# Twelve lower parts of the weights made by accumulating transfers instead of VectorE

## The chip, the cores and the metric

The kernel runs on one core of one Trainium2 chip. The metric is the device time of one launch in microseconds (us). A profile is one execution seen by the hardware profiler; its span runs from the core's first instruction to its last.

## The reference

Two layers, each on 256 tokens of width 1024. A layer normalizes its input, multiplies it by one wide input projection, feeds the columns of that product to three token mixers, projects each mixer's output to the model width, merges the three by gates and adds the result to its input:

```
h = rms_norm(x, norm_g)
proj = jnp.einsum('btd,de->bte', h, w_in)
(qa, ka, va, za, ba, aa, ub, zb, qc, kc, vc, zc, iq, ik, iw, gates) = split_columns(proj)
ya = deltanet_branch(qa, ka, va, za, ...)      # gated delta rule, short convolution on q, k, v
yb = pooling_branch(ub, zb, pool_w, pool_scale)
yc = sparse_attention_branch(qc, kc, vc, zc, iq, ik, iw, ...)
projected = jnp.einsum('btnc,ncd->btnd', branches, w_branch)
merged = jnp.sum(gate * projected, axis=2)
return x + jnp.einsum('btd,de->bte', merged, w_out)
```

All of it is float32.

## The kernel before

Large products are done in a reduced float format (`F32R`) in three products instead of one: a weight w is split into an upper part `wh` (w rounded to the reduced format) and a lower part `wl` = w - wh, the activations likewise into `hh` and `hl`, and TensorE adds up wh·hh, wh·hl and wl·hh. So each block of weights of 128x1024 float32 numbers (512 KB) passes four stations, written in `wslot`: a transfer that SyncE issues fills a buffer of `raw`; ScalarE (or VectorE) casts it into a buffer of `wh`; VectorE subtracts `wh` from `raw` into a buffer of `wl`; TensorE multiplies. There are 5 buffers of `raw`, 6 of `wh` and 5 of `wl`.

```
plan.add("ACT", "copy", (h[:, :n], raw[:, :n]), {}, ("DVE", "tensor_copy"))
V.tensor_tensor(lo[:, :n], raw[:, :n], h[:, :n].bitcast(F32), op=ALU.subtract)
```

The columns that a mixer wants with channels on the partitions go through `proj_cm`: ZC (the sparse attention's gate), KA, QA and VA (the delta rule's k, q and v), UB and ZB (the pooling mixer). Each of the six is four blocks of 128 columns; a call of `proj_cm` makes two of them in one PSUM bank of the kind `pj`. A block is 24 matmuls of 256 columns: 8 with hh,wh, 8 with hl,wh and, last, 8 with hh,wl. The calls stand in the order ZC, ZC, KA, QA, KA, QA, VA, VA, UB, UB, ZB, ZB. This part of a layer is called the channel stretch below: about 52 to 136 us in the first layer and about 320 to 411 us in the second. The other large products (`proj_tm`, `by_token`, `outp`) have 512 columns.

Nothing is issued where it is written. `Plan.add` records each operation, and `Plan.lay_out` replays all of them with a table of costs, engine by engine, and so fixes the order of each engine's queue and the buffer of each tile; it may also move a copy from ScalarE to VectorE (the last argument of `plan.add` above). A change of one operation's engine or cost therefore moves many others. On the chip each engine works its queue in that order and waits where an input is not there.

GpSimd (POOL) has little to do: some memsets, small powers (`rsqrt`, the tiles r4k, r4q, rk, so, rs) and two transfers of constants near the start. A transfer issued from it is listed under the queue POOLq.

Of the kernel before, what the change touches and what calls it, by code (L numbers as in the profile page):

```python
# [9 lines left out]
F32 = mybir.dt.float32  # L10
F32R = mybir.dt.float32r
AF = mybir.ActivationFunctionType
ALU = mybir.AluOpType
# [77 lines left out]


_slots()


def lay_w_in(w):
# [172 lines left out]
class Plan:  # L269
# [35 lines left out]
    def cost(self, eng, call, args, kw):  # L305


        out = args[0]
        n = int(np.prod(out.shape[1:])) if len(out.shape) > 1 else 1
        if call == "dma_start":  # L310
            run = int(args[1].shape[-1]) * 4
            rate = 120.0 if run < 512 else 262.0 if run < 1024 else 318.0 if run < 4096 else 338.0
            return 550.0 if eng == "POOL" else 475.0, n * out.shape[0] * 4 / rate, False
        if eng == "PE":
            if call == "transpose":
                return 109.0, 170.0, False
            if args[1].ap.dtype == F32R:
                return (n / 2.4 + 13.3 if n > 100 else 60.0), 175.0, False
            m, k = args[1].shape[-1], args[1].shape[0]
            if k <= 32:  # L320
                return 16.0, 170.0, False
            if k <= 64:
                return 58.0 * max(n / 64.0, 1.0), 170.0, False
            return 2 * (max(n, m) / 1.2 + 3), 170.0, False
        srcs = [a for a in args[1:] if isinstance(a, Ref)]
        space = [r.tile.tag.psum for r in srcs]
        ps = any(space)
        w = max([int(np.prod(r.shape[1:])) for r in srcs] + [n])
        acc = kw.get("accum_out") is not None
        if eng == "ACT":  # L330
            hold = (18 if ps else 78) + 0.875 * w
            if isinstance(kw.get("bias"), Ref) or isinstance(kw.get("scale"), Ref):
                hold += 100
            return hold + (120 if acc else 0), (95 if ps else 22) + (90 if acc else 0), False
        if eng == "POOL":
            if kw.get("op") == ALU.pow:
                return 405.0 + 151 * n, 10.0, False
            if call == "memset":
                return 50 + 0.8 * n, 50.0, False
            return 90 + 2.2 * w, 60.0, True  # L340
        if call == "reciprocal":
            return 70 + 6.0 * w, 80.0, False
        fast = call in ("tensor_copy", "tensor_scalar") and not ps and not out.tile.tag.psum
        hold = 66 + (0.52 if fast or call == "memset" else 1.045) * w
        if call in ("scalar_tensor_tensor", "tensor_scalar") and any(isinstance(a, Ref) for a in args[2:3]):
            hold += 58
        if call == "stream_shuffle":
            hold += 40
        if call == "transpose":
            hold = 464.0  # L350
        two = [r for r in ([args[1], args[2]] if call == "tensor_tensor" else
                           [args[1], args[3]] if call == "scalar_tensor_tensor" else [])]
        port = fast or (bool(two) and not any(isinstance(r, Ref) and r.tile.tag.psum for r in two))
        return hold + (65 if acc else 0), 80.0 + (30 if acc else 0), port
# [83 lines left out]
    def lay_out(self):  # L438
# [112 lines left out]
        while len(order) < len(self.ops):  # L551
            best = None
            for e in engines:
                c = pick(e)
                if c and (best is None or c[:2] < best[:2]):
                    best = c
            if best is None:
                left = [o for o in self.ops if o.start is None]
                raise RuntimeError(f"the plan is stuck with {len(left)} operations left, the first: "
                                   f"{left[0].eng} {left[0].call} {left[0].n}")  # L560
            at, e, q = best
            o = self.ops[q[1]]
            if e == "POOL" and o.other and free["DVE"] < at + PATIENCE:
                now[e] = [p for p in now[e] if p != q]
                heapq.heapify(now[e])
                soon[e] = [p for p in soon[e] if p[1:] != q]
                heapq.heapify(soon[e])
                continue
            got = slots(o)
            if got is None:  # L570
                continue
            if max(got, o.est) > at + 1e-6:
                now[e] = [p for p in now[e] if p != q]
                heapq.heapify(now[e])
                soon[e] = [p for p in soon[e] if p[1:] != q]
                heapq.heapify(soon[e])
                heapq.heappush(soon[e], (max(got, o.est), rank(o, e), o.n, o.turn))
                continue
            if o.other and e == o.other[0]:
                o.eng, o.call, o.cost, o.tail, o.port = o.other  # L580
            for t in o.tiles:
                if t.slot is None:
                    g = t.tag
                    f = min(g.free)
                    g.free.remove(f)
                    t.slot = f[1]
                    if t.slot in g.held:
                        g.held[t.slot].then = t
                    g.held[t.slot] = t
                    while g.next < len(g.order) and g.order[g.next].slot is not None:  # L590
                        g.next += 1
                    if g.free:
                        again, g.parked = g.parked, []
                        for p in again:
                            ready(p)
            if e in ("DVE", "ACT"):
                for z in o.tiles:
                    if z.tag.psum:
                        z.reader, z.until = e, at + o.cost + o.tail + 36.0
            o.start = at  # L600
            if e == "PE":
                part = fill(o) < 0.6
                free[e] = clock.run(at, o.cost + (SWITCH if part != small else 0.0), fill(o))
                if small and not part:
                    whole = at
                small = part
            else:
                free[e] = at + o.cost
            if e in shared and o.port:
                shared[e] = free[e] + (15 if e == "DVE" else 60)  # L610
            o.end = free[e] + o.tail
            if o.call == "dma_start":
                dma_free = max(dma_free, at + (2500.0 if e == "POOL" else 1360.0)) + o.tail
                o.end = dma_free + 600.0 + (DELAY if at > CALM else EARLY)
            order.append(o)
            for d in o.outs:
                d.wait -= 1
                if e == "PE" and d.eng == "PE":
                    d.est = max(d.est, at)
                else:  # L620
                    d.est = max(d.est, o.end + (35.0 if e == d.eng else self.LAG[d.eng] + (MARGIN if d.eng == "PE" else 0)))
                if not d.wait:
                    ready(d)
            for t in o.tiles:
                t.left -= 1
                t.end = max(t.end, o.end + 60)
                if not t.left:
                    g = t.tag
                    g.free.append((t.end, t.slot))
                    again, g.parked = g.parked, []  # L630
                    for p in again:
                        ready(p)
# [15 lines left out]
def trunk(ctx: ExitStack, tc: tile.TileContext, x, xt, gain, w_in, gate_b, pool_w, w_branch, w_out, cst0, cst1, cst2, cst3,  # L648
# [122 lines left out]
        G.tensor_tensor(dst, src, mhalf[:, :src.shape[-1]], op=ALU.pow)  # L771


    def wslot(src, shape, raw=None):
        n = shape[0] * shape[1]
        if raw is None:
            raw = make("raw", [128, 1024], F32)
# [1 line left out]
        h = make("wh", [128, 1024], F32R)  # L779
        lo = make("wl", [128, 1024], F32R)  # L780
        plan.add("ACT", "copy", (h[:, :n], raw[:, :n]), {}, ("DVE", "tensor_copy"))
        V.tensor_tensor(lo[:, :n], raw[:, :n], h[:, :n].bitcast(F32), op=ALU.subtract)
        return (h[:, :n].rearrange("p (k c) -> p k c", k=shape[0]),
                lo[:, :n].rearrange("p (k c) -> p k c", k=shape[0]))

# [14 lines left out]
            tabs[l, name] = c_t, s_t  # L800

    for l in range(DEPTH):
        def w_slot(key, shape):
            n = shape[0] * shape[1]
            return wslot(bass.AP(tensor=w_in.tensor, offset=w_in.offset + l * WIN + SLOT[key], ap=[[n, 128], [1, n]]),
                         shape)


        grow = grows[l]
# [71 lines left out]
        def proj_cm(c0):  # L881
            ps = bank("pj")
            o = v2(ps)
            for b in range(2):
                wh, wl = w_slot(("cm", c0 + b * 128), (8, 128))
                seq = [(w, hx, k) for w, hx in ((wh, hh), (wh, hl), (wl, hh)) for k in range(KB)]
                for n, (w, hx, k) in enumerate(seq):
                    mm(o[:, b, :], w[:, k, :], hx[:, k, :], n == 0, n == len(seq) - 1)
# [633 lines left out]
```

## Time and profile before

| | |
|---|---|
| time, median of 3 runs | 559.20 us (559.17 to 559.31) |
| time of the profiled execution | 559.21 us |
| its span | 557.4 us |
| TensorE (PE) busy | 552.3 us, 99% |
| VectorE (DVE) busy | 502.3 us, 90% |
| ScalarE (ACT) busy | 323.0 us, 58% |
| GpSimd (POOL) busy | 24.4 us, 4% |
| data moved | 99.79 MB, 179 GB/s |

The profiled execution took 1.8 us more than its span, which lies ahead of and behind the instructions. Busy shares are means over the whole span. PEld is TensorE's loading of weights into its array, which overlaps its matmuls. Idle time in a row is put down to the instruction that ended it (the releaser).

### The profile page before, as it was taken

The page shows a single profiled execution, that of the slowest core. Times are in us where ns is not written, and L with a number is a line of the kernel's source. Part 1 is how long each engine was busy: PE and PEld are TensorE (multiplying, and loading weights), DVE is VectorE, ACT ScalarE, POOL GpSimd, SP SyncE. Part 2 cuts the span into 40 slices and gives each one's busy share as a digit, 9 for nine tenths or more (in the row PEclk, how much of TensorE's full clock was granted, in tenths as well). Part 3 has the DMA queues.
Part 4 walks back from the last instruction along what each step waited for, and adds up shares of the span by engine and source line. Part 5 has one row for each costly group of instructions (what it writes and reads, how often), then busy time and mean ns, then how long its engine had stood idle before and what let it go on. Part 6 is the DMA issues. An engine that isn't in the chain of part 4 may idle for free.

```text
span 557.4 us, 9530 instructions
## 1 busy us (share of the span) xinstructions
PE 552.3 (99%) x3430; PEld 485.7 (87%) x3430; DVE 502.3 (90%) x1115; ACT 323.0 (58%) x654; POOL 24.4 (4%) x31
## 2 busy tenths in 40 slices
PE   9999999999999999999999999999999999999997
PEld 7978999999888887888879789999988888788886
DVE  6999999999999999687699999999999999967662
ACT  7795775867654526553476765765584444445530
POOL 0300000001000000000010020001000000000000
PEclk9999999999999999999999999999999999999999
DMA  8854565471866654534447446436456666346402
GB/s 327 312 194 152 186 205 183 126 268 49 308 210 194 230 181 161 199 132 152 149 142 231 138 144 202 141 127 225 133 183 215 202 207 213 119 149 208 156 33 76
DMA packets 29855, 99.79 MB, mean 179 GB/s; under 512 B 3312, under 2 KB 4080, under 8 KB 29808
## 3 DMA queue, kind: packets, MB, share of 16 engines
q1 hardware_dynamic: 29232, 98.22, 53.2%
q0 software_dynamic: 288, 0.64, 0.4%
q8 instruction: 27, 0.44, 0.3%
q10 hardware_dynamic: 288, 0.33, 0.2%
q14 instruction: 20, 0.16, 0.1%
HBM read 98.12 MB, written 1.05 MB: 178 GB/s over the span
## 4 chain that ended last, share of the span: by engine, by line
PE 89%; DVE 7%; issue 1%; ACT 1%; DMA 1%; POOL 0%; DVEq 0%; POOLq 0%
PE pj L643 72%; PE mx L643 17%; DVE u L643 2%; DVE wl L643 1%; DVE score L643 1%; DVE big L643 1%; DVE top L643 1%; DMA x_sb<-in_xt_dram 1%; ACT big L643 1%; POOL rk L643 0%; ACT wh L643 0%; DVE hl L643 0%; DVE x_sb L643 0%; ACT u L643 0%; ACT hh L643 0%
## 5 line engine op out<-in xcount | busy, mean ns | idle before, releaser
L643 ACT CAST wh<-raw 128x1024 fp32r<-128x1024 f32 (+2 forms) x165 | 170.7, 1040 | 133.0 <-PE pj L643 104.7
L643 DVE TENSOR_TENSOR wl<-raw,wh 128x1024 fp32r<-128x1024 f32 (+2 forms) x176 | 209.1, 1198 | 9.9 <-PE pj L643 5.3
L643 PE MATMUL pj<-wh,hh 128*128 128x512 f32 (+1 forms) x352 | 103.2, 391 | 0.3 <-ACT wh L643 0.3
L643 PE MATMUL pj<-wh,hl 128*128 128x512 f32 (+1 forms) x352 | 101.6, 389 | 0.0
L643 PE MATMUL pj<-wl,hh 128*128 128x512 f32 (+1 forms) x352 | 100.8, 386 | 0.0
L643 PEld LDWEIGHTS pj<-wh,hh 128*128 128x128 f32 x352 | 64.6, 188 | 13.5 <-issue 0.7
L643 PEld LDWEIGHTS pj<-wl,hh 128*128 128x128 f32 x352 | 65.1, 188 | 12.9 <-DVE wl L643 0.6
L643 PEld LDWEIGHTS pj<-wh,hl 128*128 128x128 f32 x352 | 64.8, 188 | 12.2 <-DVE hl L643 0.4
L643 PE MATMUL pj<-hh,wl 128*128 128x256 f32 x384 | 56.3, 285 | 0.0
L643 PE MATMUL pj<-hh,wh 128*128 128x256 f32 x384 | 55.3, 285 | 0.0
L643 PE MATMUL pj<-hl,wh 128*128 128x256 f32 x384 | 55.3, 285 | 0.0
L643 PE MATMUL pj<-wh,y 128*128 128x512 f32 (+1 forms) x208 | 51.5, 383 | 0.0
L643 PEld LDWEIGHTS pj<-hh,wl 128*128 128x128 f32 x384 | 50.3, 192 | 0.0
L643 PEld LDWEIGHTS pj<-hh,wh 128*128 128x128 f32 x384 | 50.2, 192 | 0.2
L643 PEld LDWEIGHTS pj<-hl,wh 128*128 128x128 f32 x384 | 49.9, 192 | 0.0
L643 PEld LDWEIGHTS pj<-wh,y 128*128 128x128 f32 x208 | 38.5, 188 | 7.5
L643 PE MATMUL mx<-wh,y 128*128 128x512 f32 (+1 forms) x128 | 38.4, 380 | 0.0
L643 PEld LDWEIGHTS mx<-u,u 128*128 128x128 f32 (+2 forms) x336 | 29.1, 164 | 3.0 <-issue 1.1
L643 PE MATMUL mx<-u,u 128*128 128x128 f32 (+2 forms) x336 | 30.7, 250 | 0.0
L643 DVE SCALAR_TENSOR_TENSOR u<-pj,cs,u 128x255 f32<-128x255 f32 (+2 forms) x72 | 29.3, 470 | 0.4 <-ACT u L643 0.4
L643 PE MATMUL pj<-wl,y 128*128 128x512 f32 (+1 forms) x104 | 28.5, 382 | 0.0
L643 PEld LDWEIGHTS mx<-wh,y 128*128 128x128 f32 x128 | 23.3, 188 | 4.4 <-DVE y L643 0.2
(202 smaller groups left out, 682.3 us busy)
## 6 DMA issues: line engine op xcount, KB each, us to landing
raw<-in_w_in_dram SPq DMA_DIRECT2D x124, 512.0 KB, 4.2
raw<-in_w_branch_dram SPq DMA_DIRECT2D x24, 512.0 KB, 4.4
raw<-in_w_out_dram SPq DMA_DIRECT2D x16, 512.0 KB, 3.5
tg<-in_gate_b_dram SPq DMA_DIRECT2D x12, 256.0 KB, 4.8
raw<-in_w_in_dram SPq DMA_DIRECT2D x4, 498.0 KB, 6.1
raw<-in_xt_dram SPq DMA_DIRECT2D x4, 256.0 KB, 4.2
raw<-in_xt_dram SPq DMA_DIRECT2D x2, 512.0 KB, 5.8
x_sb<-in_x_dram SPq DMA_DIRECT2D x2, 512.0 KB, 5.0
```

Source lines behind the costliest of these rows:

```text
L643: getattr(self.real[o.eng], o.call)(*[put(a) for a in o.args], **{k: put(v) for k, v in o.kw.items()})
```

## The change

In each of the six channel projections the last block of four is prepared in another way, twelve blocks in all over the two layers. ScalarE writes the negated weights into the buffer of the lower part; since that buffer has the reduced format, what arrives is the negated upper part. Then POOL issues a transfer from `raw` into that buffer that adds to what stands there: -wh + w = wl. VectorE's subtraction is left out for these blocks. The cast into `wh` stays. The table of costs gets a rate and a delay for such a transfer.

```diff
+def adds(l, block):
+    return block % 4 == 3
...
-            rate = 120.0 if run < 512 else 262.0 if run < 1024 else 318.0 if run < 4096 else 338.0
+            rate = 180.0 if kw.get("accum_op") is not None else 120.0 if run < 512 else 262.0 if run < 1024 else 318.0 if run < 4096 else 338.0
...
-                o.end = dma_free + 600.0 + (DELAY if at > CALM else EARLY)
+                o.end = dma_free + 600.0 + (DELAY if at > CALM else EARLY) + (1500.0 if o.kw else 0.0)
...
-    def wslot(src, shape, raw=None):
+    def wslot(src, shape, raw=None, adding=False):
...
-        V.tensor_tensor(lo[:, :n], raw[:, :n], h[:, :n].bitcast(F32), op=ALU.subtract)
+        if adding:
+            S.activation(lo[:, :n], raw[:, :n], AF.Copy, scale=-1.0)
+            G.dma_start(lo[:, :n], raw[:, :n], accum_op=ALU.add)
+        else:
+            V.tensor_tensor(lo[:, :n], raw[:, :n], h[:, :n].bitcast(F32), op=ALU.subtract)
...
-                wh, wl = w_slot(("cm", c0 + b * 128), (8, 128))
+                wh, wl = w_slot(("cm", c0 + b * 128), (8, 128), adds(l, c0 // 128 + b))
```

Counted over the whole program, VectorE has 12 subtractions of 128x1024 fewer (166 to 154) and 5 casts `wh<-raw` of 128x1024 more (10 to 15), and a few smaller copies more; ScalarE has the 12 negations and 5 such casts fewer (156 to 151), and those smaller copies fewer; POOL has the 12 transfers. TensorE has the same matmuls in another order.

POOL's queue in the first layer's channel stretch held this before (r4q and rk are small powers that wait for VectorE):

```order
L643 TENSOR_TENSOR r4q0_156<-se40_142,mhalf0_126 128x4
L643 TENSOR_TENSOR r4q1_157<-se41_143,mhalf0_126 128x4
L643 TENSOR_TENSOR rk0_185<-ssk0_180,mhalf0_126 128x4
L643 MEMSET u4_100 32x8x32
L643 TENSOR_TENSOR rk0_185<-ssk0_180,mhalf0_126 128x4
```

and holds this now:

```order
L648 TENSOR_TENSOR r4q0_156<-se40_142,mhalf0_126 128x4
L648 DMA wl2_76<-raw3_66 128x1024
L648 TENSOR_TENSOR r4q1_157<-se41_143,mhalf0_126 128x4
L648 DMA wl2_76<-raw0_63 128x1024
L648 DMA wl0_74<-raw2_65 128x1024
L648 DMA wl4_78<-raw3_66 128x1024
L648 DMA wl2_76<-raw1_64 128x1024
L648 TENSOR_TENSOR rk0_185<-ssk0_180,mhalf0_126 128x4
L648 DMA wl3_77<-raw2_65 128x1024
L648 TENSOR_TENSOR rk0_185<-ssk0_180,mhalf0_126 128x4
```

The six transfers (ZC, KA, QA, VA, UB, ZB in this order) stand among the small powers, two of which now come behind a transfer.

ScalarE's queue where the blocks of KA and QA are prepared, around the exponentials of the attention (big1 with nb1), was before:

```order
L643 ACTIVATE f1_95<-pj1_116 128x512
L643 CAST wh4_72<-raw0_63 128x1024
L643 CAST wh5_73<-raw1_64 128x1024
L643 CAST wh0_68<-raw2_65 128x1024
L643 ACTIVATE big1_112,sm41_177<-big1_112,nb1_175,r4q1_157 128x256 x4
L643 CAST wh2_70<-raw3_66 128x1024
L643 ACTIVATE big1_112<-big1_112,ri1_179 128x256 x4
```

and is now:

```order
L648 ACTIVATE f1_95<-pj1_116 128x512
L648 ACTIVATE big1_112,sm41_177<-big1_112,nb1_175,r4q1_157 128x256 x4
L648 ACTIVATE wl2_76<-raw0_63 128x1024
L648 ACTIVATE big1_112<-big1_112,ri1_179 128x256 x4
L648 ACTIVATE wl0_74<-raw2_65 128x1024
L648 COPY u1_97<-mx1_120 128x512
L648 CAST wh0_68<-raw3_66 128x1024
```

The two negations stand behind four exponentials each or more; three of the casts have gone to VectorE.

TensorE's queue at the end of KA and the start of QA (pj0 is KA's second pair, pj1 QA's) was before:

```order
L643 MATMUL pj0_115<-hl0_80,wh3_71 128x256 x7
L643 MATMUL pj0_115<-hh0_79,wl3_77 128x256 x8
L643 MATMUL pj1_116<-hh0_79,wh4_72 128x256 x8
L643 MATMUL pj1_116<-hl0_80,wh4_72 128x256 x8
L643 MATMUL pj1_116<-hh0_79,wl4_78 128x256 x8
```

and is now:

```order
L648 MATMUL pj0_115<-hl0_80,wh3_71 128x256 x8
L648 MATMUL pj1_116<-hh0_79,wh4_72 128x256 x6
L648 MATMUL pj0_115<-hh0_79,wl2_76 128x256 x8
L648 MATMUL pj1_116<-hh0_79,wh4_72 128x256 x2
L648 MATMUL pj1_116<-hl0_80,wh4_72 128x256 x8
```

Six matmuls of the next bank have been put ahead of the eight that read the lower part made by a transfer.

## Rows read from the trace of the kernel before

**Rows 1.** The page: span, busy time by engine, VectorE's busy tenths in 40 slices.
```profile
span 557.4 us, 9530 instructions
...
PE 552.3 (99%) x3430; PEld 485.7 (87%) x3430; DVE 502.3 (90%) x1115; ACT 323.0 (58%) x654; POOL 24.4 (4%) x31
...
DVE  6999999999999999687699999999999999967662
```

**Rows 2.** Busy time by stretch: the two channel stretches, the first one cut at 112.
```profile
core 0: us, PE busy (x) PEld busy (x) DVE busy (x) ACT busy (x) POOL busy (x), PEclk, DMA share, GB/s
...
52.00:112.00 60.00, 59.80 (x497) 59.21 (x496) 59.90 (x137) 41.18 (x85) 1.77 (x2) 1.00 0.51 169
112.00:136.00 24.00, 23.74 (x199) 23.53 (x199) 23.43 (x65) 15.82 (x39) 3.02 (x3) 1.00 0.43 149
...
320.00:411.00 91.00, 91.00 (x733) 89.36 (x732) 89.03 (x193) 58.76 (x125) 5.79 (x5) 1.00 0.48 157
```

**Rows 3.** Waits of TensorE's weight loads for VectorE: us, times, longest.
```profile
PEld mx L643 <- DVE u L643: 1.4, 4, 0.4
...
PEld mx L643 <- DVE y L643: 0.7, 3, 0.2
...
PEld pj L643 <- DVE wl L643: 0.6, 3, 0.2
...
PEld pj L643 <- DVE hl L643: 0.4, 1, 0.4
```

**Rows 4.** Waits of ScalarE's casts for TensorE, and of SyncE's queue for VectorE.
```profile
ACT wh L643 <- PE pj L643: 104.7, 87, 4.5
...
SPq L643 <- DVE wl L643: 325.8, 119, 15.8
```

**Rows 5.** Chain that ended last, first layer: start us, us, what.
```profile
114.64 2.27 DVE wl L643 x2
...
118.08 1.13 DVE wl L643
```

**Rows 6.** TensorE's timeline behind that chain: start us, us, what, idle before.
```profile
135.68 0.66 PE L643 MATMUL mx<-cs,u 128*128 128x128 f32 x4 [0.26 <-ACT u L643]
```

**Rows 7.** Groups by shape, VectorE then ScalarE: count, busy us, mean ns, idle before.
```profile
L643 DVE TENSOR_TENSOR wl<-raw,wh 128x1024 fp32r<-128x1024 f32 x166 | 200.1, 1215 | 9.2 <-PE pj L643 5.3 <-issue 2.0 <-PE mx L643 1.8
L643 DVE CAST wh<-raw 128x1024 fp32r<-128x1024 f32 x10 | 6.8, 683 | 0.3 <-PE pj L643 0.2
...
L643 ACT CAST wh<-raw 128x1024 fp32r<-128x1024 f32 x156 | 163.7, 1052 | 132.7 <-PE pj L643 104.4 <-issue 13.2 <-DMA raw<-in_w_in_dram 8.0
L643 ACT ACTIVATE tg<-tg 128x512 f32<-128x512 f32 x24 | 15.1, 630 | 6.3 <-DVE tg L643 6.3
```

**Rows 8.** TensorE's timeline, blocks of the channel stretch.
```profile
100.23 1.12 PE L643 MATMUL pj<-hh,wl 128*128 128x256 f32 x8
...
103.11 1.12 PE L643 MATMUL pj<-hh,wl 128*128 128x256 f32 x8
...
106.00 1.12 PE L643 MATMUL pj<-hh,wl 128*128 128x256 f32 x8
```

**Rows 9.** ScalarE's timeline, the four exponentials.
```profile
73.09 0.58 ACT L643 ACTIVATE f<-pj 128x512 f32<-128x512 f32 x1
...
79.46 0.60 ACT L643 ACTIVATE big<-big,nb,r4q 128x256 f32<-128x256 f32 x1 [0.97 <-DVE nb L643]
...
81.81 1.03 ACT L643 CAST wh<-raw 128x1024 fp32r<-128x1024 f32 x1
```

**Rows 10.** Transfers: issues, KB each, median us from issue to landing.
```profile
raw<-in_w_in_dram SPq DMA_DIRECT2D x124, 512.0 KB, 4.2
...
cs<-in_cst_dram POOLq DMA_DIRECT2D x1, 557.0 KB, 6.2
...
sgr<-in_cst_dram POOLq DMA_DIRECT2D x1, 64.0 KB, 4.3
```

**Rows 11.** POOL's timeline: a transfer's issue, and three small powers.
```profile
20.63 0.71 POOL L643 DMA_DIRECT2D cs<-in_cst_dram  x1
...
51.55 1.01 POOL L643 TENSOR_TENSOR r4q<-se,mhalf 128x4 f32<-128x4 f32 x1 [27.17 <-DVE se L643]
70.14 1.21 POOL L643 TENSOR_TENSOR r4q<-se,mhalf 128x4 f32<-128x4 f32 x1 [17.58 <-DVE se L643]
...
130.20 1.72 POOL L643 TENSOR_TENSOR rk<-ssk,mhalf 128x4 f32<-128x4 f32 x1 [6.96 <-DVE ssk L643]
```

More of the change, by code (lines that the diff above doesn't have):

```diff
@@ L802, in trunk, with w_slot @@
     for l in range(DEPTH):
-        def w_slot(key, shape):
+        def w_slot(key, shape, adding=False):
             n = shape[0] * shape[1]
             return wslot(bass.AP(tensor=w_in.tensor, offset=w_in.offset + l * WIN + SLOT[key], ap=[[n, 128], [1, n]]),
-                         shape)
+                         shape, adding=adding)
         grow = grows[l]
```

## The prediction

> **What bounds the kernel now.** I read the page first. TensorE is busy 552.3 of 557.4 us, VectorE 502.3, ScalarE 323.0 [rows 1]: the end is set by TensorE, and VectorE, which the change relieves, is the next in line. Then the busy times by stretch, because the change touches the channel stretches alone. In the first one both engines are full: TensorE 59.80 of 60 us and VectorE 59.90 of 60 up to 112, TensorE 23.74 and VectorE 23.43 of 24 behind that. In the second one TensorE is busy 91.00 of 91 us and VectorE 89.03 [rows 2]. So TensorE's idle time that a lighter VectorE could give back is 0.20 + 0.26 = 0.46 us, all in the first layer.
>
> A busy TensorE can hide short waits, since the ends of its matmuls are modelled. So I read the waits of its weight loads as well. Those for VectorE come to 1.4 + 0.7 + 0.6 + 0.4 = 3.1 us over the whole program [rows 3]; that is the most that VectorE's lateness costs TensorE in any place.
>
> Two other waits say which engine the rest waits for. ScalarE's casts of weights wait 104.7 us for TensorE to give buffers back [rows 4]: upper parts are ready ahead of their use, and the buffers, not the casts, set their pace. SyncE's loads wait 325.8 us for VectorE's subtractions, since these are the last readers of `raw` [rows 4].
>
> **The cost of each part.** Removed: 12 subtractions of 1.215 us on VectorE, 14.6 us. The plan then gives VectorE 5 more casts of 0.683 us, 3.4 us [rows 7], and some smaller copies; so about 11 us of VectorE's 502.3 are left as relief at most, 5.5 us a layer. That lies in stretches where TensorE has 0.46 us of idle time to give back, and VectorE's late chain ends there: around 114 to 119 us two of its steps are subtractions, 2.27 and 1.13 us [rows 5], and TensorE's 0.26 us of idle time at 135.68 stands at the end of that chain [rows 6]. I take half of the 0.46, a gain of 0.2 us; the bounds are 0 and 3.1.
>
> Added on ScalarE: 12 negations of 1024 columns. No row shows one; the nearest are the cast of the same size, 1.052 us, and an ACTIVATE of half the columns, 0.630, twice which is 1.26 [rows 7]. I take 1.05, as the shape and the type written are the cast's: 12.6 us, less 5 casts that left, 5.3. ScalarE is busy 41.18 of 60 us and 58.76 of 91 in these stretches [rows 2], so it costs nothing where it stands in time; what stands behind a negation (a cast, a drain of a bank) is at most 1.05 us later, and the casts have the slack of the 104.7 us.
>
> Added on POOL: 12 transfers that read `raw` and the negated part and write the sum. No row shows one. POOL's two transfers give the nearest price: 64 KB in 4.3 us, 557 KB in 6.2 [rows 10], so 493 KB take 1.9 us, and a plain copy of 512 KB from POOL would land 4.3 + 448/493 x 1.9 = 6.0 us behind its issue. An adding one reads twice as much. If the second read takes the time of the first, it is 6.0 + 2.0 = 8.0; if write and reads follow each other with no overlap at all, 10.0. I take 8.0 and keep 6.0 and 10.0 as bounds.
>
> Is there room for that? The lower parts have 5 buffers, and TensorE takes a new block every 2.88 us (100.23, 103.11, 106.00 [rows 8]), of which the lower part is read in the last 0.96. A buffer is free from its last use until the use five blocks later: 5 x 2.88 - 0.96 = 13.4 us, and small matmuls of the mixers between the blocks only widen it. Into it must fit ScalarE's way to the negation, the negation, 1.05, and the transfer, 8.0. That leaves 4.3 us for ScalarE. The worst places are KA and QA, where four exponentials stand ahead in its queue: from 79.46 to 81.81, 2.35 us, and a 0.58 us activation before them [rows 9], 2.9 in all. So 2.9 + 1.05 + 8.0 = 12.0 of 13.4: hidden, with 1.4 us to spare. A transfer becomes visible there at 9.4 us. At places with only a drain or two ahead (about 1 us) it is 11.3. At KA the queue of TensorE has moreover been bent, six matmuls of 0.12 us ahead of the lower part's.
>
> The raw buffers are held until a transfer lands instead of until the subtraction ends. Before, they also waited for a VectorE that was full (the longest such wait of SyncE is 15.8 us [rows 4]), so I cost this at nothing; the cover is the loads' own lead. DMA engines: the share is 0.51 and 0.48 [rows 2]; six transfers a stretch of 2 to 4 us each, worked out above, add 12 to 24 us to 84 or 91, at most 0.28, so loads of 4.2 us [rows 10] still fit.
>
> POOL's powers now stand behind transfers. An issue takes 0.71 us [rows 11]; the power that comes next is late by that, plus by what the transfer waits for ScalarE's negation. The one on a chain is the power rk at 130.20, which lasts 1.72 us [rows 11]: 0.7 us there could eat the gain of 0.2 and add a few tenths. I leave it at 0, since the chain also loses subtractions.
>
> The sum: 559.21 for the profiled execution, which is the runs' median of 559.20, less 0.2: **559.0 us**.
>
> **The rivals.** *The transfer is longer than its room (slower).* One mechanism: an adding transfer over 9.4 us makes TensorE wait for `wl` at KA and QA, four blocks in the two layers, and over 11.3 at all twelve. At 10.0 it costs 4 x 0.6 = 2.4 us, 561.6; at 12 it would be 4 x 2.6 + 8 x 0.7 = 16 us, 575. For it speaks that no adding transfer stands in the trace; against it, that 8.0 already counts a second read in full. Chance 0.20.
>
> *VectorE holds POOL up (slower).* POOL must write a transfer's descriptors, and the same power on POOL takes 1.01 us at one time and 1.72 at another [rows 11], in stretches where VectorE is full: something holds POOL for up to 0.7 us. If each transfer is held by two of VectorE's casts of 0.683 us, of which there are now more, 8.0 becomes 9.4, the point at which it shows; with a third, 10.1, 0.7 us at four blocks, 2.8 us, 562.0. Against it: the 557 KB transfer was issued at 20.63 [rows 11], in the second of the page's 40 slices, where VectorE is at 9 tenths or more [rows 1], and still landed in 6.2 us. Chance 0.12.
>
> The Trainium skill, "SBUF — State Buffer", section "SBUF: two separate sides", has this as a rule: a transfer issued from GpSimd needs descriptors written there, and VectorE's copies in their two-port mode lock GpSimd out of the port, 620 ns becoming about 3100. By that rule alone each transfer could come some 2.5 us later, 10.5 us, and cost 4 x 1.1, or 4.4 us: 563.4. The trace of before cannot show it for a transfer of this kind; its powers show a smaller hold.
>
> *VectorE was the bound (faster).* If the relief takes away half of the 3.1 us of VectorE-made waits, 557.7; all of it, 556.1. For it speaks that VectorE is full in these stretches and its steps lie on the chain there [rows 5]; against it, that TensorE is full as well, and the chain costs it 0.26 us of idle time [rows 6]. Chance 0.17.
>
> *The relief is eaten.* The plan puts casts back on VectorE, which stays near full; the time is that of my forecast, and so it is counted in it.
>
> **How the numbers follow.** A change of 0.2%, 1.1 us, is about what a measurement of this kernel can tell from none. My forecast, 558.1 to 560.3, has 0.51. Slower: 0.20 + 0.12 = 0.32, most of it from 560.5 to 564. Faster: 0.17, most of it from 557 to 558. The range from 557.4 to 564.0 leaves out the last part of the faster case (0.06) and transfers of 11 us and more (0.10).
>
> **What would show it.** In the changed profile: VectorE's busy time down by 5 to 12 us, ScalarE's up by 3 to 8, POOL's twelve issues with a median to landing of 6 to 9 us, and next to no waits of the weight loads pj for the transfers. TensorE's busy time in the two stretches stays at full. The prediction is wrong if landings take over 9.4 us and TensorE idles ahead of matmuls with hh,wl, or if TensorE's steps in the channel stretch get closer together than the trace of before leaves room for. It would also be wrong if the new order, which differs in many places outside these blocks, opened waits of its own elsewhere.

## The result, and the profile after

The changed kernel takes 562.66 us (median of 6 runs, 561.57 to 564.43) against 559.26 us of the kernel before (6 runs, 559.17 to 559.36): 0.62% slower, ratio 1.0062, 95% interval 1.0049 to 1.0074. The profiled execution took 562.51 us with a span of 560.7, 3.3 us longer than before [rows 1]. The runs also scatter more: over 2.9 us, before over 0.2 (over 1.0 to 1.2 us in the 16 to 33 runs of the kernel before that stand beside the experiments).

The page of the changed kernel: span, busy time by engine, and the queue (packets, MB, share of 16 DMA engines) that holds the adding transfers:

```profile
span 560.7 us, 9546 instructions
...
PE 552.7 (99%) x3430; PEld 485.7 (87%) x3430; DVE 495.8 (88%) x1118; ACT 323.8 (58%) x651; POOL 34.8 (6%) x43
...
q0 software_dynamic: 2016, 6.93, 6.5%
```

TensorE does the same work in a longer span (552.7 us busy, 552.3 before), and VectorE is relieved by 6.5 us, so the loss is idle time of TensorE. The stretches of [rows 2], after (columns as there):

```profile
52.00:112.00 60.00, 58.50 (x485) 57.78 (x485) 58.57 (x146) 41.34 (x85) 6.42 (x7) 1.00 0.68 197
112.00:136.00 24.00, 24.00 (x203) 24.00 (x202) 22.23 (x68) 15.62 (x36) 4.07 (x4) 1.00 0.68 235
320.00:411.00 91.00, 90.26 (x718) 88.23 (x717) 83.98 (x195) 58.13 (x124) 10.90 (x11) 1.00 0.64 194
```

TensorE, which missed 0.20 us in the first stretch, now misses 1.50, and 0.74 in the third, which was full; what the second one now lacks comes just behind its end, at 137.97. The view of TensorE's own waits tells for what. First the kernel before, then the changed one (us, times, longest):

```profile
...
PE pj L643 <- ACT wh L643: 0.3, 1, 0.3
PE mx L643 <- ACT u L643: 0.3, 1, 0.3
PE mx L643 <- ACT big L643: 0.2, 1, 0.2
```

```profile
PE mx L648 <- ACT big L648: 1.5, 1, 1.5
PE mx L648 <- ACT u L648: 1.2, 1, 1.2
...
PE pj L648 <- DMA wl<-raw: 0.7, 1, 0.7
PE pj L648 <- ACT wh L648: 0.3, 1, 0.3
```

The row left out in both is a wait of 1.1 us at the start. Three waits are new or longer: 1.3 + 0.9 + 0.7 = 2.9 of the 3.3 us. Only one of them is for an adding transfer; two are for ScalarE, in the mixers' small matmuls. What stands behind each is read from the chain that leads up to it.

The first, at 71.85 us (TensorE's timeline, then the chain, then ScalarE's timeline):

```profile
71.85 0.33 PE L648 MATMUL mx<-cs,big 128*128 128x128 f32 x1 [1.50 <-ACT big L648]
```

```profile
62.84 7.58 DMA raw<-in_w_in_dram
...
70.45 1.05 ACT wh L648
```

```profile
70.45 1.04 ACT L648 CAST wh<-raw 128x1024 fp32r<-128x1024 f32 x1 [1.03 <-DMA raw<-in_w_in_dram]
71.40 1.28 ACT L648 ACTIVATE big<-big,ri 128x128 f32<-128x128 f32 x4
```

A load that SyncE issued at 62.84 took 7.58 us, where 4.2 was usual [rows 10]. Its cast on ScalarE waited 1.03 us for it, and behind the cast in the same queue stood the four scalings of `big` for which TensorE waited. The load was issued 0.4 us behind ZC's adding transfer (62.48). The second, at 137.97, has the same head (rows of the chain):

```profile
108.04 7.78 DMA raw<-in_w_in_dram
...
115.90 1.05 ACT wh L648
...
117.27 1.75 ACT u L648 x9
...
137.04 0.88 ACT u L648 x3
...
137.97 1.01 PE mx L648 x7
```

Here UB's transfer had been issued 1 us ahead of the load, at 107.02; VectorE's chain between these rows carries the delay of 115.90 on to 137. The third, in the second layer, is ZC's transfer itself:

```profile
332.27 9.82 DMA wl<-raw
...
342.14 1.22 PE pj L648 x8
```

And yet the transfers are short as a rule. The lines of the view by tile on their issue (ns, least, median, most) and landing:

```profile
L648 POOL DMA_DIRECT2D wl<-raw x12: 842/873/1204, 62.5 to 398.0; - x12
...
DMA to landing us min/median/max: 4.5/5.3/9.8
```

Nine land within 4.5 to 7.2 us and make no wait of TensorE. The three that land at 9.2, 8.6 and 9.8 us are the ones of the three places above.

### The profile page after: what moved, and what is told of

Same layout as the page of the kernel before. It is cut to its first block, busy times and chain, and to the rows that moved or that the text cites. A ratio compares the mean times of both kernels' runs of the same rounds, so it can differ in the third digit from the quotient of the medians.

```text
span 560.7 us, 9546 instructions
## 1 busy us (share of the span) xinstructions
PE 552.7 (99%) x3430; PEld 485.7 (87%) x3430; DVE 495.8 (88%) x1118; ACT 323.8 (58%) x651; POOL 34.8 (6%) x43
## 3 DMA queue, kind: packets, MB, share of 16 engines
HBM read 98.12 MB, written 1.05 MB: 177 GB/s over the span
## 4 chain that ended last, share of the span: by engine, by line
PE 79%; DVE 12%; DMA 5%; ACT 2%; issue 2%; DVEq 0%; SPq 0%; ACTq 0%; POOLq 0%
PE pj L648 63%; PE mx L648 16%; DVE u L648 4%; DMA raw<-in_w_in_dram 3%; DVE wl L648 3%; DMA wl<-raw 2%; DVE score L648 1%; DVE big L648 1%; DVE y L648 1%; ACT u L648 1%; DMA x_sb<-in_xt_dram 1%; DVE top L648 1%; ACT wh L648 1%; ACT big L648 1%; DVE hl L648 0%
## 5 line engine op out<-in xcount | busy, mean ns | idle before, releaser
L648 ACT CAST wh<-raw 128x1024 fp32r<-128x1024 f32 (+2 forms) x160 | 165.2, 1039 | 118.6 <-PE pj L648 91.4
L648 DVE TENSOR_TENSOR wl<-raw,wh 128x1024 fp32r<-128x1024 f32 (+2 forms) x164 | 195.2, 1198 | 17.0 <-PE pj L648 9.8
L648 PE MATMUL pj<-wl,hh 128*128 128x512 f32 (+1 forms) x352 | 102.0, 388 | 0.0
```

The lines of the kernel that those rows point to most:

```text
L648: getattr(self.real[o.eng], o.call)(*[put(a) for a in o.args], **{k: put(v) for k, v in o.kw.items()})
```

## The experiments

The theory formed from this: an adding transfer costs time only where it is issued into a burst of weight loads; there it and the loads slow each other on the DMA engines, and either the transfer itself or a block loaded beside it is late. Rivals: the new order of the queues makes the waits; GpSimd's transfers are held up by VectorE; every transfer costs a share; and, as from the start, that VectorE's relief is worth something.

**Runs 1 to 3: the same order, less to transfer.** In the loop that issues the planned operations the changed kernel got, one edit a run:

```diff
+            args = [a[:, :64] for a in o.args] if o.call == "dma_start" and o.kw else o.args      # e1: 64 of 1024 columns
+            args = [a[:, :512] for a in o.args] if o.call == "dma_start" and o.kw else o.args     # e2: 512 columns
+            kw = {} if o.call == "dma_start" else o.kw                                            # e3: copies, adds nothing
```

> The order of the changed kernel, instruction for instruction, but each of the twelve adding transfers moves 64 of the 1024 columns (32 KB in place of 512), so twelve lower parts are wrong but for these columns. Theory (collision): the 3.3 us come from the transfers and the loads slowing each other on the DMA engines. Then the landings fall to about 4 us with no one over 6, loads in the channel stretches land in 5.5 us or less, the three waits of TensorE at 71.9, 138.0 and 342.1 shrink to those of before (0.2, 0.3 and 0 us), and the time is 559.0 to 559.7. Rival (new order): the planner's new order makes ScalarE late whatever the transfers move. Then the first two waits stay at 1.5 and 1.2 us and the time is 561.5 to 562.7. Rival (VectorE holds POOL): the landings of the transfers at 62, 107 and 332 us stay at 8 us or more, although they move next to nothing.

> As e1, with 512 of the 1024 columns moved (256 KB). Collision: between e1 and the changed kernel, 559.7 to 561.5, with the landings in bursts of loads at 6 to 7.5 us. New order: 561.5 to 562.7 as before it. VectorE holds POOL: no different from e1.

> The order of the changed kernel, the twelve transfers moving all 512 KB but copying instead of adding (the twelve lower parts are then the weights themselves, so the output is wrong). It tells what the adding costs beside the moving. If the second read is what fills the DMA engines, landings alone fall from 5 us to about 4 and in bursts from 9 to 7, and the time is 560 to 561.3; if the moving alone does it, landings and time stay as in the changed kernel, 561.5 to 563.

**Run 4: the relief without transfers.** The kernel before, with no lower parts made for the twelve blocks; TensorE reads `wh` a second time in their place, and there is no transfer. The planner lays everything out anew, so this run has the relief and another order together.

```diff
-        lo = make("wl", [128, 1024], F32R)
+        lo = h if adding else make("wl", [128, 1024], F32R)
...
+        if not adding:
+            V.tensor_tensor(lo[:, :n], raw[:, :n], h[:, :n].bitcast(F32), op=ALU.subtract)
```

> The kernel before, with the twelve lower parts left out and nothing in their place: TensorE reads the upper part a second time, so the products lack the twelve lower parts. It bounds what VectorE's relief can give. By my prediction's step the relief is worth 0.2 us: 558.6 to 559.4. By the rival that VectorE was the bound, up to 3.1 us: 556.1 to 558.

Measured against the kernel before on the same chip (559.24 us):

| run | us | ratio, 95% | transfers: median landing |
|---|---|---|---|
| e1_small | 559.12 | 1.0000 (0.9991 to 1.0008) | 2.7 us |
| e2_half | 559.55 | 1.0009 (1.0000 to 1.0018) | 3.7 us |
| e3_copy | 559.88 | 1.0013 (1.0004 to 1.0022) | 3.8 us |
| e4_free | 559.75 | 1.0008 (0.9999 to 1.0017) | none |

With 64 columns the time is that of before: the order of the queues, the negations, the issues on POOL and the bent queue of TensorE cost nothing that the interval of 0.09% either way would show. That rules out the new order, and it rules out VectorE holding POOL up in the writing of descriptors, as far as that does not grow with the columns, since the twelve transfers are still issued beside a VectorE of 496.0 us. TensorE's waits in e1_small:

```profile
...
PE mx L649 <- ACT big L649: 0.3, 1, 0.3
PE pj L649 <- ACT wh L649: 0.3, 1, 0.3
```

The landings were not quite as low as the theory had put them: one transfer of 32 KB still landed at 6.9 us and one load took 6.3, where at most 6 and 5.5 had been expected.

In e1_small the loads also show that it is not the longer hold on the buffers of `raw` that makes the first two places late. The two late loads were issued 0.4 and 1.0 us behind their transfers there too (62.74 and 106.81), and then took this long (transfers listed for windows at these two issues):

```profile
raw<-in_w_in_dram SPq DMA_DIRECT2D x1, 512.0 KB, 5.3
```

```profile
raw<-in_w_in_dram SPq DMA_DIRECT2D x1, 512.0 KB, 4.5
```

In the changed kernel they took 7.58 and 7.78.

e2_half came out at 559.55 and e3_copy at 559.88, both lower than the theory had put them: the loss does not grow in step with the bytes. The same bytes without the addition cost 0.13%, a fifth of the 0.62. The lines of the software queue in e3_copy and in the kernel before say what the addition adds:

```profile
q0 software_dynamic: 2016, 6.93, 3.5%
```

```profile
q0 software_dynamic: 288, 0.64, 0.4%
```

(3.5 - 0.4)% of a span of 559.0 us over twelve is 1.4 us of all 16 DMA engines for a plain copy of 512 KB; in the changed kernel (6.5 - 0.4)% of 560.7 over twelve is 2.9 us. The adding transfer occupies the engines twice as long. In e3_copy's profiled execution, the slowest of its eleven at 560.77, TensorE waits 1.2 us for `big` at the first place; at the two others it waits 0.2 us at most.

e4_free takes 10 us off VectorE (492.4 us busy) and wins nothing: a gain of over 0.01% lies outside its interval. By itself that could be a gain which the new order ate. But TensorE's two idle times that a lighter VectorE was to give back, 0.20 and 0.26 us before, are 0.29 and 0.28 in its profile, so the relief did not shorten them.

**Where there is room.** e1_small has the changed kernel's order with next to nothing to transfer, so it shows what the DMA engines have left at each place. Its windows of 9 us from five of the twelve issues (columns as in [rows 2], DMA share next to last):

```profile
62.30:71.30 9.00, 8.66 (x73) 8.41 (x73) 8.78 (x21) 6.78 (x17) 1.97 (x2) 1.00 0.82 270
...
95.10:104.10 9.00, 9.00 (x77) 9.00 (x76) 9.00 (x18) 7.84 (x13) 0.84 (x1) 1.00 0.43 121
105.70:114.70 9.00, 9.00 (x78) 9.00 (x77) 9.00 (x16) 6.16 (x18) 0.84 (x1) 1.00 0.81 265
...
329.70:338.70 9.00, 9.00 (x78) 9.00 (x77) 9.00 (x19) 4.88 (x6) 0.90 (x1) 1.00 0.89 273
...
355.10:364.10 9.00, 9.00 (x78) 9.00 (x77) 8.47 (x15) 3.58 (x7) 0.83 (x1) 1.00 0.28 75
```

At the three places of the waits the share is 0.82, 0.81 and 0.89: 1.6, 1.7 and 1.0 us of all engines free, less than the 2.9 that a transfer wants. At eight of the other nine it is 0.19 to 0.61, at least 3.5 us free. The ninth, QA of the first layer, has 0.83; its transfer took 7.2 us and the loads beside it up to 6.8, with no wait of TensorE.

**Runs 5 and 6: which of the twelve.** The same loop, with the transfers counted (0, 4 and 6 are ZC and UB of the first layer and ZC of the second):

```diff
+            if o.call == "dma_start" and o.kw:
+                if nth in (0, 4, 6):          # e5; in e6: nth not in (0, 4, 6)
+                    args = [a[:, :64] for a in args]
+                nth += 1
```

> The order of the changed kernel; the three transfers that met bursts of loads (ZC of both layers, UB of the first; they landed 9.2, 9.8 and 8.6 us behind their issue) move only 64 of the 1024 columns, the other nine are whole. Left out: the correct lower part in 960 columns of three blocks. Collision theory (the loss sits where a whole adding transfer is issued amid four or more loads): 559.1 to 559.9, transfers at 4.5 to 6 us, TensorE's waits for big and u back at 0.2 to 0.4 us each. Rival (every adding transfer costs its share, about 3.3/12 us): 559.2 + 9 x 0.28 = 561.7.

> The mirror image: only those three transfers are whole, the other nine move 64 columns. Left out: the correct lower part in 960 columns of nine blocks. Collision theory: 561.3 to 562.7, the three land at 8 to 10 us, TensorE waits 1 us or more for big and for u. Rival (shared loss): 559.2 + 3 x 0.28 = 560.0.

Before on that chip: 559.05 us. e5_nine, with nine whole transfers, takes 559.27 us, ratio 1.0005 (0.9996 to 1.0013); e6_three, with the three, 561.91, ratio 1.0051 (1.0039 to 1.0063). So the three carry 0.51 of the 0.62%, the nine at most 0.13, and a loss shared by all (561.7 and 560.0) is excluded in both. Two of the nine landed later than the 6 us that the theory allowed, at 7.4 and 6.9, and one of the three a little earlier than its 8, at 7.8. The waits of TensorE that answer to it, in e6_three:

```profile
PE pj L654 <- ACT wh L654: 1.1, 1, 1.1
...
PE mx L654 <- ACT u L654: 1.1, 1, 1.1
PE pj L654 <- DMA wl<-raw: 0.5, 1, 0.5
PE mx L654 <- ACT big L654: 0.4, 1, 0.4
```

The waits for `u` and for the transfer are back; the one for `big` is only 0.4, where 1 us or more had been expected. (This profiled execution is one of 563.2 us, above its median: its wait of 1.1 for `wh` stands near the program's start, where nothing was changed.)

**Runs 7, 9 and 10: through which queue a late load reaches TensorE.** In the order of the changed kernel, as it is issued, the cast of the late block goes behind the four scalings of `big` (e7_swap); in e10_both_queues the subtraction that needs this cast also goes behind VectorE's copy of `u`. Else every queue is the same:

```diff
 ScalarE, both:
-CAST wh2<-raw2
 ACTIVATE big3<-big3,ri0 x4
+CAST wh2<-raw2
 VectorE, e10_both_queues only:
-TENSOR_TENSOR wl1<-raw2,wh2
 TENSOR_SCALAR bad1<-score1
 SCALAR_TENSOR_TENSOR z0<-f0,pj0
 COPY u13<-mx1
+TENSOR_TENSOR wl1<-raw2,wh2
```

> The changed kernel with one exchange in ScalarE's queue: the cast of the block whose load landed late (70.45 in the changed kernel, 1.03 us of waiting for its load) stands behind the four scalings of big instead of ahead of them; every other queue is the same. Theory (a late load costs TensorE because the cast that waits for it stands ahead of the mixer's work in ScalarE's queue): TensorE's wait of 1.50 us for big at 71.85 falls to 0.3 or less, the load still lands at 7 to 8 us, and the time is 1.0 to 1.4 us lower, about 561.3 where the changed kernel takes 562.6. Rival (TensorE would soon have waited for that block's own weights anyway): the wait only moves to wh or wl of that block, and the time stays at 562.3 to 562.9.

> The changed kernel itself, beside the next two on the same chip, so that they are compared with it directly: 562 to 563.3 by every theory, as its earlier runs took 561.6 to 564.4.

> The changed kernel with the late block's work taken out of the way in both queues: the cast of wh stands behind the four scalings of big on ScalarE, and the subtraction that needs this cast stands behind the copy of u on VectorE (three rows later). Everything else is as in the changed kernel; the exchange on ScalarE alone took the wait for big away but a wait of 1.73 us for u came up 2.3 us later. Theory (a load that lands late stops whatever stands behind its cast and behind its subtraction, in both queues): both waits gone, TensorE's gaps at 70 to 75 us back to 0.5 us in all, 1.0 to 1.5 us less than the changed kernel on this chip. Rival (TensorE soon needs this block itself): a wait for wh or wl of the block at 75 to 79 us and no gain, within 0.4 us of the changed kernel.

e7_swap took 563.80 us, ratio 1.0080 (1.0067 to 1.0093), not less than the changed kernel but rather more (one of its six runs took 1940.6 us and stands outside the ratio; there is no profile of it, and its cause is open). The wait for `big` was gone, and another stood at 74.67. TensorE's timeline and VectorE's:

```profile
74.67 1.16 PE L660 MATMUL mx<-u,u 128*128 128x128 f32 x8 [1.73 <-DVE u L660]
```

```profile
71.99 1.23 DVE L660 TENSOR_TENSOR wl<-raw,wh 128x1024 fp32r<-128x1024 f32 x1 [1.91 <-ACT wh L660]
...
73.93 0.68 DVE L660 COPY u<-mx 128x512 f32<-128x512 f32 x1
```

VectorE's subtraction waited for the postponed cast, and the copy of `u` behind it was late instead. Neither the theory, which saw only ScalarE's queue, nor its rival, a wait for the block's own parts, had this.

e10_both_queues took 562.54 us, ratio 1.0056 (1.0044 to 1.0069), beside 562.28 of the changed kernel itself on that chip (e9_after_again, ratio 1.0053, 1.0040 to 1.0066; before 558.99). The gain of 1.0 to 1.5 us that was expected did not come. In its profile TensorE has no wait from 69 to 79 us, but then one of 0.80 for the next mixer's `big`:

```profile
81.56 0.44 PE L662 MATMUL mx<-cs,big 128*128 128x128 f32 x2 [0.80 <-ACT big L662]
```

In the same profile the waits for `u` and for the transfer are 1.5 and 1.2 us, so that the three come to 3.5 us, as the changed kernel's do (1.5 + 1.2 + 0.7). Two profiles of one and the same kernel suggest why so little could be won. The execution of e9_after_again has only 0.4 us at the first place and 1.4 at the third:

```profile
PE pj L648 <- DMA wl<-raw: 1.4, 1, 1.4
PE mx L648 <- ACT u L648: 1.2, 1, 1.2
...
PE mx L648 <- ACT big L648: 0.4, 1, 0.4
```

Its cast of the first place found its load there (ScalarE's timeline; no wait at 69.25), and its transfer of the third took 10.48 us (chain):

```profile
69.25 1.05 ACT L648 CAST wh<-raw 128x1024 fp32r<-128x1024 f32 x1
70.21 1.28 ACT L648 ACTIVATE big<-big,ri 128x128 f32<-128x128 f32 x4
```

```profile
331.19 10.48 DMA wl<-raw
```

So how long a transfer or a load takes in a burst differs from run to run, and the wait with it. The 1.5 us of the first profile need not be what the first place costs in the median (e6_three, with the same transfer there, has 0.4 as well), and e10 may have tried to win back what is mostly not there. What the first place is worth stays open between 0.4 and 1.5, and how much of the scatter of 2.9 us comes from it.

**Runs 8 and 11: without the three.** The three blocks go back to VectorE, and the planner lays all out anew; e11_fewer_small is the same with 64 columns.

```diff
 def adds(l, block):
-    return block % 4 == 3
+    return block % 4 == 3 and block != 39 and (l, block) != (0, 19)
```

> The changed kernel in which the three blocks whose transfers met the bursts (ZC of both layers, UB of the first) have their lower parts made by VectorE again, and the planner lays everything out anew; nine transfers stay. Nothing is left out. Collision theory: 559.2 to 560.5, since nine landings at 5 us fit their room, and since the relief of VectorE was worth nothing; over 560.5 if the new plan puts another transfer among four loads, which the landings would show (8 us or more). Rival (shared loss): 561.7.

> The version with nine transfers and the plan made for them (560.29 us), its transfers cut to 64 of 1024 columns. Left out: the correct lower part in 960 columns of nine blocks. If what that version loses, 1.2 us against the kernel before, is the two transfers of KA and QA among four loads (8.4 and 9.3 us there): 559.0 to 559.5, the wait of 0.9 us for u at 136.3 gone. If it is its plan (the power rk of 2.2 us, VectorE's order): 560.0 to 560.5 and the wait stays.

e8_fewer takes 560.29 us, ratio 1.0025 (1.0015 to 1.0035), and e11_fewer_small 560.37, ratio 1.0024 (1.0015 to 1.0033). Both have the same wait (the line of e11_fewer_small):

```profile
PE mx L649 <- ACT u L649: 0.9, 1, 0.9
```

In this version the transfers cost nothing, though three of its nine land at 8.4 to 9.3 us, for which the theory had expected more than 560.5: a slow landing costs only where a queue that TensorE waits for has no slack. So e8_fewer came out within the theory's 559.2 to 560.5, but not for its reason; its loss of 1.2 us is that of its plan. The longer wait for `u` (0.3 before) is some 0.6 of it; which of the many rows that the planner moved makes it was not tried. No version beat the kernel before.

## Why the prediction was wrong, point by point

**The step that failed** is the one on the DMA engines: "six transfers a stretch of 2 to 4 us each, worked out above, add 12 to 24 us to 84 or 91, at most 0.28", so that loads would still fit beside a share of 0.51 and 0.48. Its sizes were right: a transfer takes 2.9 us of all engines, and the share of the first stretch rose by 0.17. What failed is that it set them against a mean over 60 and 91 us. Loads come in bursts, and the trace of before already showed it, in shorter windows (kernel before, columns as in [rows 2]):

```profile
62.00:72.00 10.00, 9.80 (x83) 9.60 (x82) 9.90 (x20) 6.84 (x17) 1.21 (x1) 1.00 0.91 320
...
332.00:342.00 10.00, 10.00 (x87) 10.00 (x87) 10.00 (x20) 5.20 (x6) 0.00 (x0) 1.00 0.83 284
```

At both of ZC's places 0.9 and 1.7 us of all engines were free for 2.9. UB's could not be read so: there the window 107 to 116 had 0.53 before, with 0.88 from 112 to 122, and the new order put four loads into it, as e1_small's 0.81 shows. In place of "loads of 4.2 us still fit" the runs showed six loads of 7.6 to 9.3 us beside these three transfers, and 0.51 of the 0.62% from the three alone (e6_three).

**VectorE's relief**, 0.2 us with bounds 0 and 3.1, showed in no run, and 0.2 is less than the runs can tell from 0. The upper bound was a misreading. The 3.1 us of weight loads waiting for VectorE [rows 3] were added up over the whole program, and none of them lies in a channel stretch. The waits of the weight loads in the kernel before, all that the view has from 52 to 136 us:

```profile
PEld mx L643 <- ACT u L643: 0.5, 1, 0.5
PEld mx L643 <- ACT big L643: 0.4, 1, 0.4
```

From 320 to 411 us it has none. VectorE's stand at 5 to 10 us, at 217 to 282 and at 478 to 536, where none of the twelve blocks stands; in e4_free those for `u`, `y`, `hl` and `wl` still come to 3.3. So the faster rival falls.

**The negation**, 1.05 us on ScalarE, took 1.06 (median 1058 ns), and e1_small, which kept it, lost nothing. ScalarE's busy time rose by 0.8 us, less than the 3 to 8 foretold, since other work had left it.

**The adding transfer by itself** was mis-sized: 8.0 us with a lower bound of 6.0 and a foretold median of 6 to 9, where seven of the nine outside the bursts landed in 4.5 to 5.3 us and the median of all twelve was 5.3, so that even the lower bound was too high. The plain copy, 6.0 by my row, lands at 2.9 at the least and 3.8 in the median; the step from 64 KB to 557 KB of constants [rows 10] was taken near the start, where the DMA engines are busy (8 tenths in the page's first slices), and is no price of a transfer by itself. In the bursts it took 8.1 to 10.5 us in the two profiles of the changed kernel. One number could not serve for both.

**The room.** At KA and QA, the places that I held for the worst, the transfers landed in 4.5 to 7.2 us, and nothing waited: right. At ZC of the second layer TensorE waited although the landing, 9.82 us, was below the 11.3 at which I expected to see it. Issue at 332.27, need at 341.2 (the matmuls before start at 340.28 and take 0.96): 9.0 us. The "five blocks" of room were fewer there, since two of the five `wl` buffers, this one among them, held the gates' parts until the matmuls of `sgr`:

```profile
329.68 1.18 PE L648 MATMUL mx<-wl,sgr 128*128 128x512 f32 x4
```

**POOL's powers** behind the transfers: rightly left at 0, as e1_small has the same queue. **The raw buffers** held until a landing: SyncE waited 9.2 us for them in all, four times; at the first two places they are not what made the loads late (e1_small above); what else they cost was not tried.

**The rivals.** "The transfer is longer than its room" is right in its mechanism for one place of twelve, 0.7 and 1.4 us in the two profiles. The rest of the loss came through loads of other blocks, which no rival had. "VectorE holds POOL up" falls as a cause of the loss: at VA of the first layer VectorE is full, 9.00 of 9 us in e1_small's window from 95.10 above, and in the changed kernel the whole transfer there landed in 5.3 us. By the Trainium skill's rule ("SBUF — State Buffer", section "SBUF: two separate sides") VectorE's two-port copies would lock GpSimd out from writing descriptors, by an estimate from that page's figures some 2.5 us a transfer. No run here shows a hold of that size: the twelve issues took 0.84 to 1.20 us. The longest, at 350.44, is the one across which a cast on VectorE lay (350.87 to 351.56), so a hold of up to 0.36 us may have been there; its transfer landed in 5.3 us and nothing waited. The time lay in the range, but the sign was put on the wrong side, with 0.32 on slower.

Two slips of the sums change nothing: 24 of 84 is 0.29, and of the rivals' times 561.6 and 562.0 are counted from 559.2, 563.4 and 575 from 559.0.

## What to carry to other kernels

Before adding a transfer, ask for the DMA share in a window of its own length from its issue, not for a stretch's mean: here 2.9 us of all engines fitted where the share was 0.61 or less and mostly not where it was over 0.8. A transfer that lands in time can still cost, through the loads beside it; and a late load stops whatever stands behind its first user in that engine's queue, then behind the user of that. Add up an engine's waits only over the stretches that the change touches. And take the work away altogether first (as in e4_free): if that wins nothing and the waits stay, moving the work has little to win; where a planner makes a new order each time, an order alone can cost 1.2 us (e8_fewer), so look at the waits and not only at the time.

## What was not expected of the hardware

An addition in the transfer doubles its time on the DMA engines (2.9 against 1.4 us of all 16 for 512 KB), and lengthens its landing by 1.5 us in the median (5.3 against 3.8). Even a transfer of 32 KB, which lands in 2.1 us at the least, took up to 6.9 in a burst of loads. The same kernel's landing in a burst differed by 0.7 us between two executions (9.82 and 10.48), and its time scatters by 2.0 to 2.9 us over six runs, where those of the kernel before lie within 1.0 to 1.2 us over 16 to 33.
